# Weight tiles in pairs with seven block products instead of eight, and the mLSTM one head at a time, in a one-core decoder layer

## The chip, the core and the metric

The kernel runs on one core of a Trainium2 chip, as one program. The core has a matrix engine (PE in the rows; PEld is its loading of weights, which overlaps), a vector engine (DVE), a scalar engine (ACT), a general engine (POOL), and a queue engine (SP) that issues most transfers. SBUF is the working memory, PSUM holds matmul results in eight banks of 512 float32 columns by 128 partitions. The metric is the time of one execution in device microseconds; lower is better.

## The reference

One inference step of a hybrid decoder layer for 544 tokens: 512 of a new sequence and 32 new tokens of eight running sequences. In float32:

```
z = x @ w_in        # conv gates and input b, c, h; q, k, v, o; gates i, f; merge gates gc, gm
y_conv = (b * short_conv(c * h)) @ w_conv_out
h_m, C, n, m = mlstm_chunkwise(q, k, v, i, f, C0, n0, m0)     # 4 heads of 256, chunks of 128
y_m = (headnorm(h_m) * g * sigmoid(o)) @ w_m_out
x1 = layer_norm(alpha * x + (sigmoid(gc) * y_conv + sigmoid(gm) * y_m) @ w_o)
x2 = layer_norm(alpha * x1 + square(relu(x1 @ w_ff1)) @ w_ff2)
```

The width is 1024, the MLP 4096 wide. A chunk of the mLSTM takes the state matrix C (256x256) that the chunk before it left. The eight running sequences each have a C of every head that is read, used and written back, which is called the decode here.

## The kernel before, in words

All activations are held transposed: 128 features on the partitions, 8 such groups (`KT = 8`), 544 tokens along the free axis. The weights are cut into 160 tiles of 128 output features, each [128, 1024]: eight blocks of 128x128. Float32 accuracy comes from splitting every operand of the big products into a high and a low part: `wsplit_` (lines 136 to 142) loads a tile as `wr`, copies it on ACT into `wh` (L140) and subtracts on DVE into `wl` (L141). `mm` (L144 to L153) then runs, for each of the eight blocks, three products (high x high, high x low, low x high) on two halves of 272 tokens: 48 matmuls of 272 columns for a tile, all recorded at L151, into a two-bank PSUM tile `ps`.

The stages in program order are: gates and the first k tiles; q, o, v; the mLSTM of the prompt, by chunks, with the four heads inside a chunk; the decode, 32 slices `cr` of the state; the short convolution (24 tiles); its output product; the merge; the product with `w_o`; first norm; four rounds of MLP (eight tiles of the first matrix, eight of the second); second norm. A scheduler orders each engine's queue: it may interleave stages, so the mLSTM stands in the matrix engine's queue among the products of other tiles. Where a norm follows, the weights stay resident and the first half of the tokens goes through all eight tiles before the second half (`half`), so that the norm of one half has products beside it. Heads need DVE and ACT work in a chain: scores `S`, masked into `pm`, output `n` from `pm` and from the `state`, and the state's update `u`:

```
nc.vector.scalar_tensor_tensor(state[:, h, dt], state[:, h, dt],
                               dec[:, h, ch:ch + 1], pu[:, :257], op0=ALU.mult, op1=ALU.add)
```

In the decode each slice is loaded (`cr`), split (`ch` on ACT, `cl` on DVE, L492 and L493), used by matmuls `pq`, updated from matmuls `us` (L509 on DVE), and stored by a transfer that POOL issues. Six buffers of `cr` turn. POOL else does little: the mask `km`, a few products, and the low parts of eight tiles in the first round of the MLP (L141 and L611 with `eng` set to it).

Of the kernel before, what the change touches and what calls it, by code (L numbers as in the profile page):

```python
# [8 lines left out]
F32 = mybir.dt.float32  # L9
# [3 lines left out]
PSUM = bass.MemoryType.PSUM  # L13

P = 128
SEQ = 512
# [5 lines left out]
HW = 288               # tokens of the first part where the last norm follows  # L22
KT = 8
NH = 4
# [7 lines left out]
# columns of the packed small operands  # L32
# [10 lines left out]
# order of the weight tiles  # L43
W_K, W_Q, W_O, W_V, W_CONV, W_YC, W_GC, W_GM, W_OUT, W_FF = 0, 8, 16, 24, 32, 56, 64, 72, 88, 96


@with_exitstack
def tile_hybrid(ctx: ExitStack, tc: tile.TileContext, xT, wt, wg, pk, caug,
# [7 lines left out]
    wp = pool("wp", 3)  # L56
    slots = pool("slots")
    tmp = pool("tmp", 2)
    psa = pool("psa", 4, space=PSUM)
    pstate = {}  # L60

    def products_psum(n):
        """four banks for the products: two tiles of two, or four of one"""
        if pstate:
            pstate["stack"].close()
        pstate["stack"] = st = ExitStack()
        pstate["pool"] = pool(f"psm{len(pstate)}", n, stack=st, space=PSUM, reuse_waits="tile")

    ctx.callback(lambda: pstate["stack"].close())
    products_psum(2)  # L70
# [7 lines left out]
    def slot(i, pl=slots):  # L78
        return pl.tile([P, KT, NT], F32, name=f"slot{i}", tag=f"slot{i}")

    def r(ap):
        return ap.bitcast(F32R)

# [6 lines left out]
    ident = col("ident")  # L90

# [1 line left out]
    warm = cst.tile([P, P], F32, name="warm")  # L93
    nc.gpsimd.memset(warm, 0.0)
    pwm = aux("pwm")
    for j in range(9):
        nc.tensor.matmul(pwm[:, :P], warm, warm, start=True, stop=True)
    xh, xl = slot(0), slot(1)
    wgr = wp.tile([P, KT * P], F32, name="wgr", tag="wr")[:, :KT * 64]
    wgs = wp.tile([P, KT, P], F32R, name="wgs", tag="wh")  # L100
    early = {}

    def wload(i):
        raw = wp.tile([P, KT * P], F32, name=f"wr{i}", tag="wr")
        nc.sync.dma_start(raw, wt[i])
        return raw

    xr = slot(3)
    nc.sync.dma_start(wgr, wg)
    for kt in range(KT):  # L110
        nc.sync.dma_start(xr[:, kt], xT[:, kt])
        if kt == 1:
            early[0] = wload(0)
    early[1] = wload(1)
    for kt in range(KT):
        if kt == 0:
            w3 = wgr.rearrange("p (k m) -> p k m", k=KT)
            nc.scalar.copy(wgs[:, :, :64], w3)
            nc.vector.tensor_tensor(wgs[:, :, 64:], w3, wgs[:, :, :64].bitcast(F32),
                                    op=ALU.subtract)  # L120
        nc.scalar.copy(r(xh[:, kt]), xr[:, kt])
        nc.vector.tensor_tensor(r(xl[:, kt]), xr[:, kt], xh[:, kt], op=ALU.subtract)
    nc.sync.dma_start(pkt, pk)

    hv = (slice(0, HN), slice(HN, NT))

    ahead = {}

    def wsplit(i, eng=nc.vector):
        return ahead.pop(i) if i in ahead else wsplit_(i, eng)  # L130

    def split_ahead(*ii):
        for i in ii:
            ahead[i] = wsplit_(i)
# [9 lines left out]
    def mm(ps, wh, wl, ah, al, halves=hv, m=P, mid=None):  # L144
        for kt in range(KT):
            if kt == 5 and mid:
                mid()
            ws = slice(kt * m, (kt + 1) * m)
            for (w, a) in ((wh, ah), (wh, al), (wl, ah)):
                for hf, cs in enumerate(halves):  # L150
                    nc.tensor.matmul(ps[:m, hf, :cs.stop - cs.start], w[:, ws], r(a[:, kt, cs]),  # L151
                                     start=(kt == 0 and w is wh and a is ah),
                                     stop=(kt == KT - 1 and w is wl))  # L153

    def mtile(i, ah, al):
        wh, wl = wsplit(i)
        ps = pstate["pool"].tile([P, 2, 512], F32, name=f"ps{i}", tag="mm")
        mm(ps, wh, wl, ah, al)
        return ps

    def pv(ps):
        return ps[:, :, :HN]

    def hview(ap):
        return ap.rearrange("p (a n) -> p a n", a=2)

    mstk = ExitStack()          # what the mLSTM keeps to its end
# [5 lines left out]
    vk = mst.tile([P, NH, VW], F32, name="vk")  # L173
    nc.gpsimd.memset(G, 0.0)
    nc.gpsimd.memset(vk[:, :, 256:258], 0.0)
    nc.gpsimd.memset(vk[0:32, :, 256:257], 1.0)
    nc.gpsimd.memset(vk[64:96, :, 256:257], 1.0)

# [1 line left out]
    pstk = ExitStack()          # what only the prompt's mLSTM needs  # L180
    mg = pool("mg", stack=pstk)
    gstk = ExitStack()
    gr = pool("gr", stack=gstk)
    split_ahead(0, 1)
    gp = [aux(f"gp{hf}") for hf in range(2)]
    for kt in range(KT):
        for a in (xh, xl):
            for hf in range(2):
                nc.tensor.matmul(gp[hf][:, :HN], wgs[:, kt], r(a[:, kt, hv[hf]]),
                                 start=(kt == 0 and a is xh), stop=(kt == KT - 1 and a is xl))  # L190
# [4 lines left out]
    c = mg.tile([4, NT], F32, name="c")  # L195
# [5 lines left out]

    def sm(ap, n=DT):
        return ap.rearrange("p (b t) -> p b t", t=n)
# [8 lines left out]

    kT = slot(2)

    def ktile(ft):
        ps = mtile(W_K + ft, xh, xl)
        nc.scalar.activation(hview(kT[:, ft]), pv(ps), AF.Copy, scale=DH ** -0.5)

    for ft in range(3):
        ktile(ft)  # L220
# [29 lines left out]
    # rows that matmuls spread over the partitions, in exact halves: c, w_inter of the prompt  # L250
    R = mg.tile([P, SEQ], F32R, name="R")
    Rf = R.bitcast(F32)
    wrow = gr.tile([68, SEQ], F32, name="wrow")
    selr = mst.tile([P, 8], F32R, name="selr")
# [19 lines left out]
    gstk.close()  # L274
    mp = pool("mp", stack=pstk)
    E = mp.tile([P, NC, NH, P], F32, name="E")
    va = mp.tile([P, NC, NH, 257], F32, name="va")
    nc.gpsimd.memset(va[:, :, :, 256:257], 1.0)

    for ft in range(3, 6):  # L280
        ktile(ft)
# [34 lines left out]
    for ft in range(6, KT):  # L316
        ktile(ft)
# [159 lines left out]
    for t in qms:  # L477
        nc.gpsimd.memset(t, 0.0)
# [449 lines left out]
```

## Time and profile before

| | |
|---|---|
| time of three runs, us | 1104.53, 1100.12, 1102.09; median 1102.09 |
| the profiled execution, first to last instruction, us | 1099.7 |
| busy: PE, DVE, ACT, POOL, us | 1071.2, 535.5, 347.9, 143.0 |
| mean granted clock of the matrix engine, as a share of 2.4 GHz | 0.988 |
| moved by transfers | 110.37 MB, mean 100 GB/s |

The page shows no time of its own for the profiled execution beyond its span. An engine's busy time is the union of its instructions, so for the matrix engine, whose instructions overlap, the pace is read from counts over a stretch and not from the mean of one. In rows of windows an entry such as `100.00 (x800)` is the busy time of an engine and its instructions in that stretch; in rows of the timeline `x3` means three like instructions that follow each other, and the second number is the time from the first's start to the last's end.

### The profile page before, as it was taken

How to read it: one execution, taken by the hardware profiler on the slowest of the kernel's cores; microseconds unless marked ns; L12 is line 12 of the kernel's file. 1: busy time of each engine (PE TensorE's matmuls, PEld its weight loads, DVE VectorE, ACT ScalarE, POOL GpSimd, SP SyncE). 2: the span in 40 equal slices, each digit the busy share in tenths (PEclk: the TensorE clock that was granted, in tenths of full speed). 3: DMA queues.
4: the chain of work that ended last, by engine and by line, in shares of the span. 5: the costliest groups of instructions: out<-in, count | busy, mean ns of one | idle time of the engine just before them, and what ended most of it. 6: DMA issues, size and time to landing. Idle time of an engine off the chain costs nothing.

```text
span 1099.7 us, 19420 instructions
## 1 busy us (share of the span) xinstructions
PE 1071.2 (97%) x8351; PEld 1060.0 (96%) x8351; DVE 535.5 (49%) x882; ACT 347.9 (32%) x516; POOL 143.0 (13%) x161
## 2 busy tenths in 40 slices
PE   8999999999999989999999999899999999999994
PEld 8999999999999989999999999899999999999994
DVE  5533223365578778522143359742344234334576
ACT  6431222232234334213222225441233133123432
POOL 1000230000017563003200004200000000000033
PEclk9999999999999999999999999899999999999997
DMA  6222222211136775222222342112222222222201
GB/s 233 98 78 77 97 83 90 77 45 53 40 135 203 241 209 162 95 96 77 97 79 95 123 171 96 58 58 75 80 97 77 97 81 93 94 80 97 96 23 60
DMA packets 34349, 110.37 MB, mean 100 GB/s; under 512 B 3928, under 2 KB 6232, under 8 KB 34008
## 3 DMA queue, kind: packets, MB, share of 16 engines
q1 hardware_dynamic: 31704, 100.69, 28.2%
q0 software_dynamic: 2560, 8.46, 2.0%
q8 instruction: 65, 1.06, 0.4%
q14 instruction: 20, 0.16, 0.1%
HBM read 97.32 MB, written 11.81 MB: 99 GB/s over the span
## 4 chain that ended last, share of the span: by engine, by line
PE 90%; DVE 4%; DMA 3%; ACT 1%; issue 1%; POOL 0%; SPq 0%; DVEq 0%; POOLq 0%; ACTq 0%
PE ps L151 82%; DMA cr<-in_caug_dram 1%; DMA out_cs_dram<-cr 1%; PE u L419 1%; PE pq L496 1%; PE n L405 1%; DVE slot L733 1%; PE S L386 1%; PE n L402 1%; DMA wr<-in_wt_dram 1%; DVE bq L743 1%; DVE slot L671 0%; PE us L507 0%; PE ht L367 0%; PE kt L412 0%
## 5 line engine op out<-in xcount | busy, mean ns | idle before, releaser
L151 PE MATMUL ps<-slot,wh 128*128 128x272 f32 (+1 forms) x4640 | 801.2, 290 | 3.9 <-DVE slot L671 1.8
L151 PEld LDWEIGHTS ps<-slot,wh 128*128 128x128 f32 x4640 | 669.0, 189 | 7.0 <-DVE slot L671 2.5
L151 PE MATMUL ps<-slot,wl 128*128 128x272 f32 (+1 forms) x2320 | 498.2, 289 | 0.0
L151 PEld LDWEIGHTS ps<-slot,wl 128*128 128x128 f32 x2320 | 371.6, 189 | 0.7
L140 ACT CAST wh<-wr 128x1024 fp32r<-128x1024 f32 x145 | 152.1, 1050 | 501.1 <-PE ps L151 437.3
L141 DVE TENSOR_TENSOR wl<-wr,wh 128x1024 fp32r<-128x1024 f32 x142 | 174.1, 1226 | 205.8 <-ACT wh L140 201.7
L151 PE MATMUL ps<-slot,res 128*128 128x272 f32 (+2 forms) x720 | 92.8, 289 | 0.0
L151 PEld LDWEIGHTS ps<-slot,res 128*128 128x128 f32 x720 | 91.3, 188 | 0.3
L726 POOL TENSOR_TENSOR slot<-slot,bc 128x288 f32<-128x288 f32 (+1 forms) x6 | 5.8, 992 | 360.2 <-ACT bc L724 360.2
L810 DVE TENSOR_TENSOR slot<-ps,slot 128x544 f32<-128x544 f32 x16 | 11.6, 725 | 59.3 <-PE ps L151 59.3
L503 POOL TENSOR_SCALAR km<-kk,pkt 128x256 fp32r<-128x256 f32 x32 | 37.3, 1168 | 14.6 <-PE us L507 7.8
L492 ACT CAST ch<-cr 128x516 fp32r<-128x516 f32 x32 | 19.9, 623 | 49.6 <-DMA cr<-in_caug_dram 28.7
L785 ACT CAST slot<-rl 128x544 fp32r<-128x544 f32 (+1 forms) x40 | 22.2, 556 | 37.2 <-DVE rl L784 37.1
L786 DVE TENSOR_TENSOR slot<-rl,slot 128x544 fp32r<-128x544 f32 (+1 forms) x40 | 24.4, 611 | 19.6 <-ACT slot L785 19.4
L509 DVE SCALAR_TENSOR_TENSOR cr<-cr,dec,us 128x258 f32<-128x258 f32 x64 | 29.3, 475 | 3.3 <-PE us L507 3.1
L324 POOL TENSOR_SCALAR slot<-slot,pkt 128x544 f32<-128x544 f32 x8 | 16.8, 2096 | 107.9 <-ACT slot L323 107.9
L493 DVE TENSOR_TENSOR cl<-cr,ch 128x516 fp32r<-128x516 f32 x32 | 22.1, 697 | 17.6 <-ACT ch L492 17.5
L784 DVE TENSOR_TENSOR rl<-rl 128x544 f32<-128x544 f32 (+1 forms) x40 | 24.3, 607 | 11.8 <-ACT rl L783 11.8
L570 POOL TENSOR_TENSOR slot<-slot,sgc 128x544 f32<-128x544 f32 x8 | 14.5, 1809 | 88.1 <-ACT sgc L569 88.1
L783 ACT ACTIVATE rl<-ps 128x544 f32<-128x544 f32 (+1 forms) x40 | 21.2, 529 | 14.3 <-PE ps L151 14.3
L496 PE MATMUL pq<-ch,qm 128*64 128x258 f32 x64 | 18.3, 292 | 5.9 <-ACT wh L140 3.2
L141 POOL TENSOR_TENSOR wl<-wr,wh 128x1024 fp32r<-128x1024 f32 x3 | 7.3, 2423 | 124.9 <-PE am L645 121.2
(258 smaller groups left out, 715.2 us busy)
## 6 DMA issues: line engine op xcount, KB each, us to landing
wr<-in_wt_dram SPq DMA_DIRECT2D x160, 512.0 KB, 3.5
cr<-in_caug_dram SPq DMA_DIRECT2D x32, 258.0 KB, 3.9
out_cs_dram<-cr POOLq DMA_DIRECT2D x32, 258.0 KB, 3.9
slot<-in_xT_dram SPq DMA_DIRECT2D x8, 272.0 KB, 6.3
slot<-in_xT_dram SPq DMA_DIRECT2D x1, 2176.0 KB, 8.5
out_yT_dram<-slot SPq DMA_DIRECT2D x4, 288.0 KB, 2.4
out_cp_dram<-state SPq DMA_DIRECT2D x1, 1028.0 KB
out_yT_dram<-slot SPq DMA_DIRECT2D x4, 256.0 KB, 2.3
```

The source lines that it names most:

```text
L140: nc.scalar.copy(hi, raw)
L141: eng.tensor_tensor(lo, raw, hi.bitcast(F32), op=ALU.subtract)
L151: nc.tensor.matmul(ps[:m, hf, :cs.stop - cs.start], w[:, ws], r(a[:, kt, cs]), start=(kt == 0 and w is wh and a is ah), stop=(kt == KT - 1 ...
L492: nc.scalar.copy(r(chh), cr)
L493: nc.vector.tensor_tensor(r(cl), cr, chh, op=ALU.subtract)
L496: nc.tensor.matmul(pq[:2 * NS, :VW], r(qm[:, dt, bb * 2 * NS:(bb + 1) * 2 * NS]), r(part[:, dt]), start=(bb == 0 and dt == 0 and part is chh),
L503: nc.gpsimd.tensor_scalar(r(km), kk[:, 2 * h:2 * h + 2].rearrange("p a d -> p (a d)"), col("bsel")[:, bb:bb + 1], None, op0=ALU.mult)
L509: nc.vector.scalar_tensor_tensor(cr[:, dt], cr[:, dt], dec[:, h, 4 + bb:5 + bb], pu[:, :VW], op0=ALU.mult, op1=ALU.add)
L783: nc.scalar.activation(view(rl_), src, AF.Relu)
L784: nc.vector.tensor_tensor(rl_, rl_, rl_, op=ALU.mult)
L785: nc.scalar.copy(r(dh[:, ft, cs]), rl_)
L786: nc.vector.tensor_tensor(r(dl[:, ft, cs]), rl_, dh[:, ft, cs], op=ALU.subtract)
```

## The change

144 of the 160 tiles are processed in pairs. A pair is seen as a 2x2 block matrix (two output tiles by two halves of the input features), the activations as another (two halves of the features by two halves of the tokens), and the product is formed by a scheme that takes seven block products instead of eight: a block product is now 4 blocks x 3 high/low products = 12 matmuls of 272 columns, so a pair has 84 matmuls where two tiles had 96. The scheme needs sums of weight blocks (`wpair`: S1 to S4, on POOL), sums of activation blocks (`tsums`: T1 to T4, on POOL or DVE) and sums of results (`spair`, in PSUM and with ACT and DVE). Each operand is split into high and low parts after the sums. The 16 tiles of `w_o` and of the last round's second matrix stay as they were.

The activations now take 7 blocks for 4, so SBUF is laid out anew: the mLSTM runs head by head (projections of a head, `mlstm(h)`, `decode(h)`), with one buffer for most of its tiles, four for `cr`, and three PSUM banks for everything that is not a product (there were four); head outputs and gates go to DRAM and are loaded when they are merged. The low part `cl` moves from DVE to POOL, the mask `km` from POOL to ACT, the decode's stores from POOL's queue to SP's. Of the first norm only the first half has products beside it; the second half's norm is now run before the pairs of the MLP, which need all four token-by-feature blocks and their sums.

```diff
-    def wsplit_(i, eng=nc.vector):
-        raw = early.pop(i) if i in early else wload(i)
-        hi = wp.tile([P, KT * P], F32R, name=f"wh{i}", tag="wh")
-        lo = wp.tile([P, KT * P], F32R, name=f"wl{i}", tag="wl")
-        nc.scalar.copy(hi, raw)
-        eng.tensor_tensor(lo, raw, hi.bitcast(F32), op=ALU.subtract)
+    def wpair(i0, i1):
+        a, b = wload(i0), wload(i1)
+        H = KH * P
+        s = wp.tile([P, 3 * H], F32, name=f"ws{i0}", tag="ws", bufs=1)
+        s2, s1, s4 = (s[:, k * H:(k + 1) * H] for k in range(3))
+        a1, a2, b1, b2_ = a[:, :H], a[:, H:], b[:, :H], b[:, H:]
+        tt = nc.gpsimd.tensor_tensor
+        tt(s1, b1, b2_, op=ALU.add)
+        tt(s2, s1, a1, op=ALU.subtract)
+        tt(b1, a1, b1, op=ALU.subtract)
+        tt(s4, a2, s2, op=ALU.subtract)
+        g1 = halves(f"{i0}a", a)
+        g2 = halves(f"{i0}b", s[:, :2 * H])
+        g3 = halves(f"{i0}c", b)
+        g4 = halves(f"{i0}d", s4)
...
+    def tsums(nm, z, eng):
...
+        t = tmp["tt"].tile([P, 4, HN], F32, name=f"tt{nm}", tag="tt", bufs=1)
+        x1_ = z[:, 0].rearrange("p (a n) -> p a n", a=2)
+        x2_ = z[:, :, HN:]
+        eng.tensor_tensor(t[:, 0:2], x2_, x1_, op=ALU.subtract)
+        eng.tensor_tensor(t[:, 2], z[:, 1, HN:], t[:, 0], op=ALU.subtract)
+        eng.tensor_tensor(t[:, 3], z[:, 1, :HN], t[:, 2], op=ALU.subtract)
+        return t
...
+    def prod(ps, w, X, which, start):
+        set_, k = which
+        ah, al = X[set_ + "h"], X[set_ + "l"]
+        wh, wl = w
+        for kt in range(KH):
+            ws = slice(kt * P, (kt + 1) * P)
+            for n, (w_, a) in enumerate(((wh, ah), (wh, al), (wl, ah))):
+                nc.tensor.matmul(ps[:, :HN], w_[:, ws], r(a[:, kt, k]),
...
+        A = mmt(f"A{nm}")
+        prod(A, w["W11"], X, X11, True)
+        p1 = part("p1", A)
+        step()
+        F = mmt(f"F{nm}")
+        prod(F, w["W12"], X, X21, True)
+        ev.c11(F[:, :HN], p1)
+        step()
+        prod(A, w["S2"], X, T2, False)
+        q = part("q", A, 2)
+        D = mmt(f"D{nm}")
+        prod(D, w["S1"], X, T1, True)
+        prod(A, w["S3"], X, T3, False)
+        w_ = part("w", A)
+        ev.c22(D[:, :HN], w_)
+
+        def t0():
+            prod(A, w["W22"], X, T4, False)
+            ev.c21(A[:, :HN])
+
+        def t1():
+            prod(D, w["S4"], X, X22, False)
+            ev.c12(D[:, :HN], q)
+            ev.done()
...
+    for h in range(NH):
+        kT = kT0 if h == 0 else proj_k(h)
+        qT = qT0 if h == 0 else proj_q(h)
+        va, vk = proj_v(h)
+        flush()
+        mlstm(h, kT, qT, va)
+        decode(h, kT, qT, vk)
...
-        later[0], later[1] = first, second
...
+        if hf == 0:
+            later[1], later[2] = first, second
+        else:
+            Xa.update({k: o2.tile([P, KH, 4, HN], F32, name=f"a{k}", tag=k) for k in ("th", "tl")})
+            first()
+            second()
```

Here `halves` is the pair copy on ACT, subtract on DVE that `wsplit_` had, for 1024 columns (g1, g2, g3) or 512 (g4), recorded at L119 and L120 of the changed kernel; `step` runs the two last block products of the pair before. In the MLP a pair of the first matrix also squares its four results (three of them on DVE, L971) and ends with `tsplit`, the seven blocks of the next operand; a pair of the second matrix adds three partial results on POOL (L1000).

The matrix engine's queue in the mLSTM before: state updates `u` of head 0 to 3 in one chunk, with products of a weight tile (`ps`, L151) between them.

```order
L419 MATMUL u_1_1_2273<-va,kw_2249 128x257
L151 MATMUL ps_3529<-slot_87,wh_3525 128x272
L151 MATMUL ps_3529<-slot_86,wl_3526 128x272 x2
L151 MATMUL ps_3529<-slot_86,wh_3525 128x272 x2
L419 MATMUL u_2_0_2276<-va,kw_2249 128x257
L419 MATMUL u_2_1_2279<-va,kw_2249 128x257
L151 MATMUL ps_3529<-slot_87,wh_3525 128x272
L151 MATMUL ps_3529<-slot_86,wl_3526 128x272 x2
```

The same engine's queue after the change, in the mLSTM of the last head: it begins behind the last matmul of the decode of the head before (`hts`), and runs through the chunks.

```order
L629 MATMUL hts_2496<-pkt,nsbs_2478 128x32 x2
L335 MATMUL vp_0_2878<-pkt,vt_2723 128x128 x4
L507 MATMUL S_2898<-qT_2600,kT_2503 128x128 x8
L522 MATMUL n_0_2914<-va_2724,pm_2907 128x257
L539 MATMUL u_0_0_2925<-va_2724,kw_0_2917 128x257
L539 MATMUL u_0_1_2928<-va_2724,kw_0_2917 128x257
L522 MATMUL n_1_2931<-va_2724,pm_2907 128x257
L525 MATMUL n_1_2931<-state_2913,qT_2600 128x257
L539 MATMUL u_1_0_2936<-va_2724,kw_0_2917 128x257
L525 MATMUL n_1_2931<-state_2913,qT_2600 128x257
L539 MATMUL u_1_1_2939<-va_2724,kw_0_2917 128x257
```

(Rows between these that are transposes or the spread of a weight are left out.) Between the `vp` matmuls of the third head and the end of the fourth head's decode stand two products of weight tiles, and none behind those two; the queue goes on with the second pair of the convolution. By that place 1104 of the 6816 products have stood in the queue: 300 ahead of the first head's `vp`, 526 up to the second's, 276 up to the third's, and those two.

POOL's queue before, from the last product of the merge (`sgc`) to the second norm (`bc`): eight low parts of weight tiles in the first MLP round, and then nothing for the rest of the MLP.

```order
L570 TENSOR_TENSOR slot_4886<-slot_4886,sgc_5784 128x544
L141 TENSOR_TENSOR wl_7284<-wr_7281,wh_7283 128x1024
L141 TENSOR_TENSOR wl_7290<-wr_7287,wh_7289 128x1024
L611 TENSOR_TENSOR res_4_7299<-wr_7300,res_4_7299 128x1024
L611 TENSOR_TENSOR res_7_7317<-wr_7318,res_7_7317 128x1024
L726 TENSOR_TENSOR slot_6739<-slot_6739,bc_10721 128x288 x3
```

(Of the three rows of L141 two stand, of the five of L611 two.) POOL's queue after, for one pair of the first MLP matrix: the four weight sums (`ws`, and `wr` overwritten), then the sums of the hidden activations (`ttd` from `hid`).

```order
L130 TENSOR_TENSOR ws_8426<-wr_8424 128x512
L131 TENSOR_TENSOR ws_8426<-ws_8426,wr_8422 128x512
L132 TENSOR_TENSOR wr_8424<-wr_8422,wr_8424 128x512
L133 TENSOR_TENSOR ws_8426<-wr_8422,ws_8426 128x512
L152 TENSOR_TENSOR ttd_1_8372<-hid_1_8147 128x544
L153 TENSOR_TENSOR ttd_1_8372<-hid_1_8147,ttd_1_8372 128x272
L154 TENSOR_TENSOR ttd_1_8372<-hid_1_8147,ttd_1_8372 128x272
```

What moved: POOL has these seven for each such pair, where it had nothing for most of the MLP, and four for every other pair.

## Rows read from the trace of the kernel before

**Rows 1.** The page: busy time by engine, then the ending chain by engine.

```profile
PE 1071.2 (97%) x8351; PEld 1060.0 (96%) x8351; DVE 535.5 (49%) x882; ACT 347.9 (32%) x516; POOL 143.0 (13%) x161
...
PE 90%; DVE 4%; DMA 3%; ACT 1%; issue 1%; POOL 0%; SPq 0%; DVEq 0%; POOLq 0%; ACTq 0%
```

**Rows 2.** Windows: busy time (instructions) by engine, granted clock, DMA share, GB/s.

```profile
0.00:20.00 20.00, 17.15 (x100) 15.99 (x101) 9.71 (x17) 10.74 (x17) 2.94 (x22) 0.91 0.75 269
...
320.00:440.00 120.00, 114.14 (x901) 112.50 (x899) 93.92 (x201) 50.56 (x78) 65.18 (x82) 0.99 0.64 200
...
560.00:660.00 100.00, 100.00 (x800) 100.00 (x799) 41.94 (x54) 27.80 (x32) 0.00 (x0) 1.00 0.35 119
680.00:700.00 20.00, 15.72 (x93) 14.38 (x93) 19.45 (x28) 11.61 (x22) 7.74 (x4) 0.83 0.31 108
```

**Rows 3.** Groups by line and form: shapes, count, busy us, mean ns, idle before.

```profile
L141 DVE TENSOR_TENSOR wl<-wr,wh 128x1024 fp32r<-128x1024 f32 x142 | 174.1, 1226 | 205.8 <-ACT wh L140 201.7
L140 ACT CAST wh<-wr 128x1024 fp32r<-128x1024 f32 x145 | 152.1, 1050 | 501.1 <-PE ps L151 437.3 <-issue 61.5 <-DMA wr<-in_wt_dram 1.8
```

**Rows 4.** Timeline of DVE: instructions that follow each other without a wait.

```profile
551.00 1.22 DVE L141 TENSOR_TENSOR wl<-wr,wh 128x1024 fp32r<-128x1024 f32 x1
552.13 0.72 DVE L556 TENSOR_TENSOR slot<-sgm,slot 128x544 fp32r<-128x544 f32 x1
...
674.45 0.43 DVE L636 SCALAR_TENSOR_TENSOR ar0n<-av,ar0n 128x272 f32<-128x272 f32 x1
674.80 0.43 DVE L691 TENSOR_TENSOR as<-as,slot 128x272 f32<-128x272 f32 x1
```

**Rows 5.** Timeline of POOL: two instructions by themselves, two stretches beside DVE.

```profile
498.31 1.36 POOL L570 TENSOR_TENSOR slot<-slot,sgc 128x544 f32<-128x544 f32 x1 [60.10 <-ACT sgc L569]
...
665.46 2.40 POOL L141 TENSOR_TENSOR wl<-wr,wh 128x1024 fp32r<-128x1024 f32 x1 [1.07 <-ACT wh L140]
...
1074.53 2.75 POOL L726 TENSOR_TENSOR slot<-slot,bc 128x256 f32<-128x256 f32 x3 [6.52 <-ACT bc L724]
...
1087.82 2.49 POOL L759 TENSOR_TENSOR slot<-slot,bms 128x512 f32<-128x512 f32 x2 [7.08 <-ACT bms L756]
```

**Rows 6.** Timeline of DVE in the same stretches as the POOL rows.

```profile
665.65 2.50 DVE L691 TENSOR_TENSOR as<-slot 128x272 f32<-128x272 f32 x1
...
669.17 0.44 DVE L691 TENSOR_TENSOR as<-as,slot 128x272 f32<-128x272 f32 x1
...
1074.48 3.95 DVE L733 TENSOR_TENSOR slot<-slot,bc 128x256 f32<-128x256 f32 x5 [0.99 <-ACT bc L724]
...
1088.36 1.27 DVE L759 TENSOR_TENSOR slot<-slot,bm 128x512 f32<-128x512 f32 x2
```

**Rows 7.** Timeline of PE: six state-update matmul records in a row.

```profile
230.66 1.47 PE L419 MATMUL u<-va,kw 128*128 128x257 f32 x6
```

**Rows 8.** Groups by form in the mLSTM and the decode.

```profile
L493 DVE TENSOR_TENSOR cl<-cr,ch 128x516 fp32r<-128x516 f32 x32 | 22.1, 697 | 17.6 <-ACT ch L492 17.5
L492 ACT CAST ch<-cr 128x516 fp32r<-128x516 f32 x32 | 19.9, 623 | 49.6 <-DMA cr<-in_caug_dram 28.7 <-PE pq L496 8.1 <-PE ps L151 7.6
...
L424 DVE SCALAR_TENSOR_TENSOR state<-state,dec,u 128x257 f32<-128x257 f32 x24 | 10.8, 480 | 5.3 <-PE u L419 5.1
...
L389 DVE TENSOR_TENSOR pm<-S,E 128x512 f32<-128x512 f32 x4 | 2.8, 690 | 3.2 <-PE S L386 3.2
```

**Rows 9.** The page: transfers by group, KB each, median us to landing.

```profile
cr<-in_caug_dram SPq DMA_DIRECT2D x32, 258.0 KB, 3.9
out_cs_dram<-cr POOLq DMA_DIRECT2D x32, 258.0 KB, 3.9
```

**Rows 10.** Timeline of PE: matmuls behind a gap in the decode.

```profile
404.98 0.31 PE L496 MATMUL pq<-ch,qm 128*64 128x258 f32 x1 [3.16 <-ACT wh L140]
...
405.87 0.63 PE L507 MATMUL us<-vk,km 128*128 128x258 f32 x2
...
407.84 1.04 PE L151 MATMUL ps<-slot,wh 128*128 128x272 f32 x4
```

More of the change, by code (lines that the diff above doesn't have):

```diff
@@ L13 @@
 PSUM = bass.MemoryType.PSUM
+DRAM = bass.MemoryType.DRAM
 P = 128
@@ L55, in tile_hybrid @@
     cst = pool("cst")
[L56 to L70, printed above, removed]
+    wp = pool("wp")
+    stg = pool("stg")
+    o1 = pool("o1")
+    dr = pool("dr", space=DRAM)
+    psa = pool("psa", 3, space=PSUM)
+    psm = pool("psm", 5, space=PSUM)
     def tables(name):
@@ L90, in tile_hybrid @@
     ident = col("ident")
[L93 to L101, printed above, removed]
+    hD = dr.tile([P, KT, NT], F32, name="hD")
+    yD = dr.tile([P, KT, NT], F32, name="yD")
+    gD = dr.tile([P, KT, NT], F32, name="gD")
@@ L144, in mm @@
[L144 to L153, printed above, removed]
@@ new lines, in tile_hybrid, with __init__, part, add @@
+    class Evac:
+        def __init__(self, z, scale=None, done=None):
+            self.z, self.scale, self.then = z, scale, done
+        def part(self, t, ps):
+            if self.scale is None:
+                nc.scalar.copy(t, ps)
+            else:
+                nc.scalar.activation(t, ps, AF.Copy, scale=self.scale)
+        def add(self, out, ps, t):
+            if self.scale is None:
+                nc.vector.tensor_tensor(out, ps, t, op=ALU.add)
+            else:
+                nc.vector.scalar_tensor_tensor(out, ps, self.scale, t, op0=ALU.mult, op1=ALU.add)
+        def c11(self, ps, t):
+            self.add(self.z[:, 0, :HN], ps, t)
+        def c22(self, ps, t):
+            self.add(self.z[:, 1, HN:], ps, t)
+        def c12(self, ps, t):
+            self.add(self.z[:, 0, HN:], ps, t)
+        def c21(self, ps):
+            self.part(self.z[:, 1, :HN], ps)
+        def done(self):
+            if self.then:
+                self.then()
@@ L172, in tile_hybrid @@
     Es = mst.tile([NS, NH, NS], F32, name="Es")
-    vk = mst.tile([P, NH, VW], F32, name="vk")
-    nc.gpsimd.memset(G, 0.0)
[L175 to L184, printed above, removed]
-    gp = [aux(f"gp{hf}") for hf in range(2)]
[L186 to L190, printed above, removed]
+    R = mst.tile([P, SEQ], F32R, name="R")
@@ new lines, in tile_hybrid @@
+    E = mst.tile([P, NC, NH, P], F32, name="E")
+    wb = mst.tile([P, 2, NH, NS], F32, name="wb")
+    selr = mst.tile([P, 8], F32R, name="selr")
+    epst = cst.tile([P, 1], F32, name="epst")
+    hp = pool("hp", 2, stack=mstk)
+    gstk = ExitStack()
+    tmp["tt"] = gr = pool("gr", stack=gstk)
+    warm = gr.tile([P, P], F32, name="warm")
+    nc.gpsimd.memset(warm, 0.0)
+    nc.gpsimd.memset(G, 0.0)
+    nc.gpsimd.memset(epst, EPS)
+    pwm = aux("pwm")
+    for j in range(9):
+        nc.tensor.matmul(pwm[:, :P], warm, warm, start=True, stop=True)
@@ new lines, in tile_hybrid @@
+    kT0 = proj_k(0)
+    w3 = wgr.rearrange("p (k m) -> p k m", k=KT)
+    nc.scalar.copy(wgs[:, :, :64], w3)
+    nc.vector.tensor_tensor(wgs[:, :, 64:], w3, wgs[:, :, :64].bitcast(F32), op=ALU.subtract)
+    gp = [aux(f"gp{hf}") for hf in range(2)]
+    for hf, terms in enumerate((((0, X11), (KH, X21)), ((0, X11), (KH, X22), (0, T1)))):
+        seq = [(o + kt, X[s_ + hl][:, kt, k]) for o, (s_, k) in terms for kt in range(KH)
+               for hl in "hl"]
+        for n, (kt, a) in enumerate(seq):
+            nc.tensor.matmul(gp[hf][:, :HN], wgs[:, kt], r(a), start=(n == 0),
+                             stop=(n == len(seq) - 1))
@@ L272, in tile_hybrid @@
     nc.sync.dma_start(m_o, mo)
[L274 to L281, printed above, removed]
+    qT0 = proj_q(0)
     for ch in range(NC + 1):
@@ L573, in tile_hybrid @@
[L573 to L585 removed]
+    n = NU - 2
```

781 lines of the change are left out of this document (437 added, 344 removed).

## The prediction

> **What bounds the kernel now.** I read the page first: the matrix engine is busy for 1071.2 us of a span of 1099.7, and 90% of the ending chain is its own [rows 1]. DVE is at half of the span and POOL at an eighth. Then the windows [rows 2]: from 560 to 660 us 800 products start in 100 us, 125 ns each, without a gap, while POOL does nothing. So a tile's 48 products cost 6.0 us and two tiles 12.0, and what else a tile needs (a copy of 1.05 us, a subtract of 1.23 [rows 3]) is hidden. Two stretches differ. In the decode (320 to 440) the matrix engine is busy for 114 of 120 us; behind the first norm (680 to 700) it runs 93 products where 160 fit, with a granted clock of 0.83. A change that shortens products is therefore worth their count, until another engine needs longer for a pair than the products do; that is what I looked for next.
>
> The sum is made against the profiled execution's 1099.7 us. The median of the runs, 1102.1, is 2.4 more, which is added at the end.
>
> **Products.** 72 pairs have 84 products for 96: 72 x 12 x 0.125 = 108 us less. A pair's products now take 10.5 us. This is the only saving.
>
> **What DVE and POOL need for a pair.** The scheme adds POOL work, and the trace shows that POOL and DVE are not independent. By themselves, POOL took 1.36 us for 544 columns and 2.40 for 1024, and 1.245 for 512 [rows 5]: 2.4 ns a column, so 0.66 for 272. On DVE, 1024 columns with two SBUF operands take 1.13 from start to start and 272 take 0.35 [rows 4]; by the line through these, 512 take 0.60, 544 take 0.63 and 1088 take 1.20. But a DVE instruction of 272 columns that began beside a POOL product took 2.50 us: it started 0.19 after POOL's and ended 0.29 after it, where a like one took 0.44 [rows 5, 6]. And where three POOL and five DVE instructions of 256 columns ran together, POOL's took 0.92 each and DVE's 0.79 [rows 5, 6]. By the lines POOL's would be 0.61 and DVE's 0.33. A pair of them then has 0.95 us of work, and takes 0.92 at POOL's pace. So they hardly overlap. Where DVE's other operand was in PSUM it kept its pace beside POOL: two of 512 columns in 1.27 [rows 5, 6]. I therefore add the prices of POOL's instructions and of DVE's with two SBUF operands, multiply by 0.95, and compare with 10.5.
>
> The Trainium skill ("SBUF — State Buffer", section "Who interferes with whom") calls the port pair that DVE and GpSimd share an exclusive lock; the rows agree but for 0.92 against 0.95. By the lock in full, without the factor 0.95, the sum would be 30 us higher; that is rival three.
>
> A pair without other work: DVE's subtracts are three of 1024 and one of 512, 3.99 us; POOL's four sums of 512 are 4.98. Together 8.97, by the factor 8.5: hidden under 10.5.
>
> A pair of the first MLP matrix has in addition three squares of 272 (1.05), the low parts of 544, 272 and 1088 (2.18), and POOL's activation sums of 544, 272, 272 (2.68): 14.88, by the factor 14.1. Twelve such pairs (three rounds of four) are 3.6 over 10.5: **43 us**. A pair of the second matrix adds three POOL sums of 272 to the plain pair, 10.95 or 10.4: nothing over. The last round's four have no activation sums and fewer parts, about 10.6: nothing.
>
> Three convolution pairs have 26.9 for weights and 11.1 for POOL's product of 1024, four taps, the gate, low parts and sums: 38.0, by the factor 36.0, over 31.5. About three and a half of the four such groups stand behind the mLSTM, where nothing else fills the time: **15 us**. The four pairs of `o` have a product of 1088, low parts and sums: 15.0, by the factor 14.2, 15 us over; the four plain pairs of `gm` behind them give back up to 2 us each: **7 us**. The merge's four have three of 1088: 12.6, by the factor 11.9: **6 us**.
>
> This term is 71 us. Below, it is 0 if weights split ahead and the two engines' gaps absorb it; above, 101 without the factor, and 130 as an outer bound if the instructions also wait for one another in their chains.
>
> **The mLSTM head by head.** Before, the state updates of several heads stood in the matrix engine's queue among products [the first order rows]. Now 1102 of the products stand ahead of the third head's `vp`, and two behind it until the fourth head's decode ends; the next pairs need space that the mLSTM frees. So the third and fourth heads run with almost no cover. One head: the prompt's four chunks need about 21 us, some 6 to the first state (scores, mask 0.69, transposes), three further chunks of 3.2 (ten float32 matmul records of about 0.22, as six take 1.47 less the last one's tail [rows 7], and two state updates of 0.48 [rows 8]), and about 5 for head norm and transposes, six to ten steps of 0.48 to 0.69 [rows 8]. The decode has eight slices through four buffers instead of 32 through six: load 3.9 [rows 9], `ch` 0.62 [rows 8], `cl` 1.27 on POOL by its pace, matmuls and updates about 1, store 3.9 [rows 9] make a turn of 10.6 for four slices, about 20 for eight. Together 42, of which the matrix engine works about 18.5 (36 records of 0.22, some 90 smaller at 0.11 to 0.125). It idles 23.5 per head, 47 for two. The second head has 276 products (34 us) in its 42, so about 9 more. Before, the decode idled 6 [rows 2], which go. **+50 us**. Below 20, if a head's decode overlaps the next head's prompt; above 90, if the chains' steps also wait for DVE's and POOL's weight work.
>
> What the change moves without a wait of its own: the mask from POOL to ACT, the decode's stores from POOL's queue to SP's. On SP a store stands ahead of later loads of `cr` and of weights; that is within the decode's turn above. Head outputs and gates through DRAM add a few MB where the transfers move 119 GB/s in a product stretch and 269 at the start [rows 2]: nothing.
>
> **The other places.** The second half's norm now stands before the first pair of the MLP with nothing beside it. Before, 680 to 700 lost 67 of 160 products, 8.4 us [rows 2]; after, the chain of sums, root, scale, sums of blocks and split I take as 20 us: **+12**, between 5 and 25. At the start a pair needs all of `x` and two tiles, 3.3 MB at 269 GB/s [rows 2], 12 us, then four sums through one buffer: **+7**, between 2 and 15. At the four seams between the MLP's matrices the last hidden tile's squares, sums and split (about 6 us) have 58 products (7 us) beside them, which the pair's last two block products only partly are: 2 each, **+8**, between 0 and 16.
>
> Sum: -108 + 71 + 50 + 12 + 7 + 8 = +40. 1099.7 + 40 is 1139.7; with 2.4, **1142 us**, 3.6% slower.
>
> **The rivals.**
> One, faster: DVE and POOL have slack that I do not count, since weights can be split ahead during light pairs and their instructions interleave better than in the rows. For it: DVE is at 49% now and POOL at 13% [rows 1]. Against it: the 2.50 us of [rows 6]. The first term goes from 71 to 0: 1071. The kernel is faster when this term is below 31 with the others as they stand. Chance 0.2.
> Two, no change: both large terms come out at a little over half (71 to 41, 50 to 37, the start and seams hidden): about 1098 to 1103. Chance 0.08.
> Three, much slower: the clock falls in the uncovered heads, or the two engines exclude each other entirely. For the clock: behind a gap of 3.16 us two like matmuls take 0.63 and four products 1.04 to the end of the last [rows 10], so about 0.2 us from one to the next instead of 0.125, and 680 to 700 has 0.83 [rows 2], a mixture of 2.4 and 1.2 GHz. The work of the two uncovered heads, 37 us, would take twice as long: +35, so 1177. The exclusion without the factor gives +30, 1172. Chance 0.22.
> The Trainium skill ("TensorE: Matmul & The Clock Gate", section "Why this matters for your kernels") says that idle gaps between bursts of matmuls put the clock back to its lower level; rows 10 agree, and by this rule alone rival three would be the likelier.
>
> **How the numbers follow.** My forecast, 1142 with a range of its own from 1110 to 1165, has 0.5. What a measurement of this kernel can tell from no change is about 0.5%, 5.5 us. Faster by more than that is rival one, 0.2; within it is rival two, 0.08; slower is the forecast and rival three, 0.72. The range that leaves out no more than 2 in 10 reaches from 1075, near rival one, to 1200, above rival three with both of its causes in part.
>
> **What the profile after would show.** If the exclusion is right: the sums at L130 to L133 at 1.2 us or longer and DVE's subtracts at L120 well above 1.13 in their mean, both engines together near full in the MLP rounds, and a window of 100 us in them with about 620 to 700 products instead of 800. If rival one holds, the windows have 800, and POOL and DVE overlap. If the head term is right, the matrix engine idles for about 45 us between the third head's first product and the second convolution pair, waiting for DVE and for `cr`; the granted clock there decides rival three. The windows behind the first norm and at the start show the smaller terms. I would be wrong on the sign if DVE and POOL had no such stretch, and wrong on the size most likely in the heads, where no row shows a head alone.

## The result, and the profile after

The changed kernel takes **1264.3 us** (median of four runs, 1260.4 to 1266.9), the kernel before 1102.6: a ratio of **1.1475**, interval 1.1442 to 1.1508. It is nearly 15% slower. I had forecast slower by 3.6%, 1142 us, with a range up to 1200; the direction was right, the size was not, and the time lies 64 us above the range.

The page of the changed kernel: busy time by engine, then the ending chain by engine (against [rows 1]).

```profile
PE 1063.9 (84%) x7487; PEld 1009.3 (80%) x7487; DVE 917.8 (73%) x1263; ACT 566.9 (45%) x946; POOL 701.6 (56%) x488
...
DVE 11%; PE 10%; POOL 6%; issue 5%; DMA 2%; ACT 2%; DVEq 0%; POOLq 0%; ACTq 0%
```

The shares of the second line are of the whole span, and they add up to 36%: the chain's first piece begins at 813.3 us, and ahead of it nothing was followed. So its 10% is not to be set against the 90% of before; in the part that was followed, the MLP, DVE and POOL have 17% together and the matrix engine 10%. Over the whole execution DVE or POOL is busy for 1098 of 1261.5 us. The matrix engine's own busy time hardly fell (1071 to 1064) though 864 products are gone. The windows of the changed kernel (columns as in [rows 2]) show where the time goes:

```profile
0.00:40.00 40.00, 26.01 (x113) 22.68 (x114) 24.81 (x30) 16.82 (x25) 20.70 (x37) 0.68 0.38 135
250.00:338.00 88.00, 59.06 (x279) 44.59 (x278) 45.39 (x141) 30.47 (x64) 23.13 (x19) 0.77 0.37 119
366.00:476.00 110.00, 92.94 (x670) 90.42 (x669) 94.23 (x107) 48.78 (x79) 76.74 (x46) 0.94 0.23 76
576.00:597.00 21.00, 21.00 (x169) 21.00 (x168) 13.82 (x16) 11.82 (x18) 13.70 (x9) 1.00 0.39 130
786.00:845.00 59.00, 36.76 (x229) 33.74 (x228) 42.08 (x72) 29.71 (x58) 15.88 (x14) 0.80 0.10 36
915.00:1023.00 108.00, 93.04 (x671) 89.29 (x671) 79.52 (x85) 48.17 (x76) 83.47 (x56) 0.94 0.24 77
```

From 576 to 597 two pairs run their 168 products in 21 us, 125 ns each: here the scheme gives its whole 1.5 us a pair. Elsewhere it does not. Eight convolution pairs take 110 us for 84 (366 to 476). One MLP round, eight pairs, takes 108 (915 to 1023). At the start, in the third and fourth heads (250 to 338, 88 us for two) and behind the norm (786 to 845) the matrix engine is idle for 33 to 38% of the time, and its granted clock is 0.68 to 0.80.

What the weight sums cost is seen in the groups by form of the changed kernel: POOL's four sums, and one DVE line of the hidden tiles and one of the resident weights (which have no POOL sums beside them).

```profile
L133 POOL TENSOR_TENSOR ws<-wr,ws 128x512 f32<-128x512 f32 x72 | 138.4, 1922 | 0.0
L131 POOL TENSOR_TENSOR ws<-ws,wr 128x512 f32<-128x512 f32 x72 | 124.5, 1729 | 4.7
L132 POOL TENSOR_TENSOR wr<-wr,wr 128x512 f32<-128x512 f32 x72 | 116.4, 1617 | 0.0
L130 POOL TENSOR_TENSOR ws<-wr 128x512 f32<-128x512 f32 x72 | 106.4, 1478 | 295.5 <-DMA wr<-in_wt_dram 96.4
...
L971 DVE SCALAR_TENSOR_TENSOR hid<-hid 128x272 f32<-128x272 f32 x48 | 39.1, 819 | 0.8
...
L120 DVE TENSOR_TENSOR resl<-wr,resh 128x1024 fp32r<-128x1024 f32 x8 | 9.8, 1223 | 2.3 <-ACT resh L119 2.1
```

512 columns on POOL, 1.245 us unhindered [rows 5], take 1.48 to 1.92 in the mean; DVE's 272 columns, 0.44 [rows 6], take 0.82. Two stretches of the timeline of the changed kernel, DVE first, then POOL, show why:

```profile
1058.95 2.31 DVE L120 TENSOR_TENSOR wl131a<-wr,wh131a 128x1024 fp32r<-128x1024 f32 x1
1061.18 1.52 DVE L971 SCALAR_TENSOR_TENSOR hid<-hid 128x272 f32<-128x272 f32 x1
1062.63 2.39 DVE L159 TENSOR_TENSOR d2tl<-ttd,d2th 128x1088 fp32r<-128x1088 f32 x1
1064.94 2.31 DVE L120 TENSOR_TENSOR wl131b<-ws,wh131b 128x1024 fp32r<-128x1024 f32 x1
1067.17 0.43 DVE L247 TENSOR_TENSOR hid<-D,w 128x272 f32<-128x272 f32 x1
```

```profile
1058.63 1.54 POOL L130 TENSOR_TENSOR ws<-wr 128x512 f32<-128x512 f32 x1 [1.84 <-DMA wr<-in_wt_dram]
1060.25 2.15 POOL L131 TENSOR_TENSOR ws<-ws,wr 128x512 f32<-128x512 f32 x1
1062.37 1.50 POOL L132 TENSOR_TENSOR wr<-wr,wr 128x512 f32<-128x512 f32 x1
1063.83 2.33 POOL L133 TENSOR_TENSOR ws<-wr,ws 128x512 f32<-128x512 f32 x1
```

They take turns. DVE's subtract waits from 1058.95 for POOL's sum to end at 1060.17 and then runs 1.1; POOL's next sum starts at 1060.25, waits for DVE until about 1061.2 and ends at 1062.40; and so on. Only L247, whose first operand `D` is in PSUM, keeps its 0.43. Both engines are drawn as busy, and at any time one of them works.

### The profile page after: what moved, and what is told of

It is laid out like the page before. It is cut to its first block, busy times and chain, and to the rows that moved or that the text cites. A ratio compares the mean times of both kernels' runs of the same rounds, so it can differ in the third digit from the quotient of the medians.

```text
span 1261.5 us, 19444 instructions
## 1 busy us (share of the span) xinstructions
PE 1063.9 (84%) x7487; PEld 1009.3 (80%) x7487; DVE 917.8 (73%) x1263; ACT 566.9 (45%) x946; POOL 701.6 (56%) x488
## 5 line engine op out<-in xcount | busy, mean ns | idle before, releaser
L130 POOL TENSOR_TENSOR ws<-wr 128x512 f32<-128x512 f32 x72 | 106.4, 1478 | 295.5 <-DMA wr<-in_wt_dram 96.4
L133 POOL TENSOR_TENSOR ws<-wr,ws 128x512 f32<-128x512 f32 x72 | 138.4, 1922 | 0.0
L131 POOL TENSOR_TENSOR ws<-ws,wr 128x512 f32<-128x512 f32 x72 | 124.5, 1729 | 4.7
L132 POOL TENSOR_TENSOR wr<-wr,wr 128x512 f32<-128x512 f32 x72 | 116.4, 1617 | 0.0
L605 POOL TENSOR_TENSOR cl<-cr,ch 128x516 fp32r<-128x516 f32 x32 | 44.7, 1401 | 87.4 <-ACT ch L604 76.4
L241 ACT COPY p<-A 128x272 f32<-128x272 f32 x68 | 26.1, 384 | 48.5 <-PE A L183 37.4
L241 ACT COPY w<-A 128x272 f32<-128x272 f32 x68 | 25.9, 381 | 31.5 <-PE A L183 29.8
L971 DVE SCALAR_TENSOR_TENSOR hid<-hid 128x272 f32<-128x272 f32 x48 | 39.1, 819 | 0.8
L241 ACT COPY q<-A 128x272 f32<-128x272 f32 x68 | 25.9, 380 | 28.9 <-PE A L183 28.8
L152 POOL TENSOR_TENSOR ttd<-hid 128x544 f32<-128x544 f32 x12 | 25.3, 2110 | 21.8 <-DVE hid L971 19.4
L1000 POOL TENSOR_TENSOR x<-x,w 128x272 f32<-128x272 f32 x12 | 15.5, 1288 | 8.9 <-ACT w L241 8.9
```

The source lines that it names most:

```text
L130: tt(s1, b1, b2_, op=ALU.add)
L131: tt(s2, s1, a1, op=ALU.subtract)
L132: tt(b1, a1, b1, op=ALU.subtract)
L133: tt(s4, a2, s2, op=ALU.subtract)
L241: nc.scalar.copy(t, ps)
L605: nc.gpsimd.tensor_tensor(r(cl), cr, chh, op=ALU.subtract)
```

## The experiments

Each kernel is the changed one with the edit shown (in part, `...` for what is left out), unless it says otherwise. e1 to e6 and e12 ran once each. e1 to e4 are set against one run of the kernel before on the same chip, 1100.9 us, and against the changed kernel's 1264.3. The four runs of the changed kernel span 6.5 us, and the kernel before had 1099.7 to 1103.2 from chip to chip, so a difference of a few us between two single runs says nothing.

**e1: no sums of weight blocks.**

```diff
...
-        tt(s1, b1, b2_, op=ALU.add)
-        tt(s2, s1, a1, op=ALU.subtract)
-        tt(b1, a1, b1, op=ALU.subtract)
-        tt(s4, a2, s2, op=ALU.subtract)
         g1 = halves(f"{i0}a", a)
-        g2 = halves(f"{i0}b", s[:, :2 * H])
+        g2 = halves(f"{i0}b", a)
         g3 = halves(f"{i0}c", b)
-        g4 = halves(f"{i0}d", s4)
+        g4 = halves(f"{i0}d", b1)
```

> The four weight-block sums on POOL are left out (the seven block products run on plain blocks, so the outputs are not the reference's); everything else is as in the changed kernel. Theory A (POOL and DVE exclude each other, and the sum of their prices for a pair decides the pace): 72 x 4.98 = 359 us of excluded time goes, pairs of the first MLP matrix need 9.9 and convolution groups 23 us, under their products, so the waits between the heads and the first norm and in the MLP rounds go, and with them half of the slow-clock time: 1110 to 1150 us. Theory B (the waits stand at serial places, the seams between matrices, heads and norm, whatever POOL does): 1210 us or more.

Measured 1135.0: theory A. The four POOL sums of a pair cost 129 us, and A's 359 us of POOL time were two thirds hidden. One MLP round falls from 108 to 92.5 us; a window of e1 over it, to set against 915 to 1023 above:

```profile
831.00:924.00 93.00, 88.86 (x678) 86.59 (x677) 62.72 (x86) 48.77 (x77) 28.38 (x24) 0.98 0.29 93
```

From the first product of one stage to that of the next, the 129 us lie so: 21 up to the second convolution group, 25 in the convolution behind it, 7 in the yc and gc pairs, 17 in o and gm, 3 in the merge and the product with `w_o`, 46 in the first three MLP rounds and 9 from there to the end.

**e2: all sums on DVE.** `tt`, `tsums`, the added partial results (L1000) and the convolution's product (L668) get `nc.vector` for `nc.gpsimd`.

> All weight-block sums, activation sums, added partial results and the convolution's product move from POOL to DVE; nothing is left out. Theory A: DVE does them at 1.04 ns a column instead of POOL's 2.4 and nothing excludes it any more; a pair of the first MLP matrix then has 12.0 us on DVE alone (3.99 + 2.4 + 1.05 + 2.18 + 1.33 + 1.05) instead of 14.9 of both and 1.05 of PSUM adds, a plain pair 7.4: 1150 to 1190 us. Rival (DVE is simply the fuller engine, and POOL's work beside it is a help): DVE gets some 200 us more, and the time rises above 1264.

Measured 1163.2: theory A, 101 us faster with the same arithmetic. It is not POOL's slowness by itself that cost them: by my prices POOL alone needs 4.98 + 2.68 us for a pair of the first MLP matrix, 7.7, under the products' 10.5. In the groups of e2 DVE makes a sum in 0.68 to 0.71 us, and its 272 columns are back at 0.43:

```profile
L131 DVE TENSOR_TENSOR ws<-ws,wr 128x512 f32<-128x512 f32 x72 | 51.3, 712 | 0.4
...
L971 DVE SCALAR_TENSOR_TENSOR hid<-hid 128x272 f32<-128x272 f32 x48 | 20.3, 433 | 0.1
```

**e3: the layout with eight products.** Everything but the scheme: each pair multiplies its two plain tiles, and `t` holds the split of the fourth activation block instead of four sums.

```diff
+        def out(tag, k, c):
+            ps = mmt(f"{tag}{nm}")
+            prod(ps, w[f"W{k}1"], X, X11 if c == 1 else X12, True)
+            prod(ps, w[f"W{k}2"], X, X21 if c == 1 else X22, False)
+            return ps[:, :HN]
```

> The new layout and order alone: head by head, gates and head outputs through DRAM, second half of the first norm in front of the MLP, but each pair with its eight block products (96 matmuls) and no sums; nothing is left out of the result. Theory A: the layout alone loses in heads, norm, start and their slow clock some 75 to 100 us against the kernel before, 1175 to 1205 us, so that seven products save 108 and cost some 170 to 195 in DVE and POOL work and what follows from it. Rival (the layout is free, the scheme costs everything): within 15 us of 1102.

Measured 1163.7, 62.7 above the kernel before; 11 below A's window, far from the rival. A window of e3 over an MLP round:

```profile
851.00:947.00 96.00, 96.00 (x766) 96.00 (x765) 37.72 (x56) 29.88 (x48) 0.00 (x0) 1.00 0.27 89
```

Eight pairs of 96 products in 96.6 us, with no wait at the seam between the matrices. Counted as time beyond 125 ns a product, e3 loses 157 us up to its fifth convolution pair (at 343 us), behind all its heads, and the kernel before 105 up to the end of its decode (at 440): 52 more, the start included. Behind that e3 loses 10 more, 8 of them around the first norm. So the layout's 62.7 lie mostly in the heads and the norm, and the scheme, which takes 864 products (108 us) away, made the kernel 100.6 us slower on top of it.

**e4: the gate pairs in the fourth head.** The eight pairs of `gc` and `gm` are written in `decode`'s place of the fourth head, results through DRAM.

```diff
         mlstm(h, kT, qT, va)
+        for j in more[2 * h]:
+            gate_pair(j)
+        flush()
         decode(h, kT, qT, vk)
+        for j in more[2 * h + 1]:
+            gate_pair(j)
```

> The eight pairs of the two merge gates stand in the fourth head, two sets of four, both results through DRAM, so that products stand among the third and fourth heads' matmuls; arithmetic as in the changed kernel. Theory A: the heads' waits (9.8 + 12 + 9.1 us in 240 to 360) and the slow clock of their own matmuls (some 28 us over before) mostly go: 1205 to 1225 us. Rival (in the heads DVE is the bound, and products there only move the wait): 1245 us or more.

Measured 1238.5, 26 us less, between the two theories. The matrix engine is better filled from 240 to 390, but the seams ahead of the yc pairs and of the merge, where the same pairs had stood, got longer (from the first product of the last o pair to that of the second merge pair 36.9 us, where the products of two pairs need 21).

**e5: e2 and e4 together.**

> The second and fourth experiment together: all sums on DVE, and the eight gate pairs in the fourth head. Theory A (two separate losses): the 25 us of the gate pairs come off the 1163 of the DVE sums, 1130 to 1145 us. Rival (DVE is the bound in the heads as soon as it makes the sums): 1155 us or more.

Measured 1153.8: only 9 under e2, just below the rival's window. The gains do not add; with DVE's sums the gate pairs bring a third of what they brought.

**e6: a pair of the next round in each seam.** On e5.

```diff
+        if ck < 3:
+            z0 = ztile(f"hid{ck + 1}_0")
+            spair(i0 + 16, i0 + 16 + KH, Xa, Hidden(z0))
```

> As e5, and the first pair of the next MLP round stands ahead of each second matrix of the rounds one to three, so that 84 products that need nothing of the last hidden tile lie in the seam. Theory A (a round's loss of 10 us over its eight pairs' 84 is the wait for the last hidden tile's split and sums): rounds of 85 to 88 us instead of 94, 15 to 25 us under e5. Rival (DVE's work for a round sets its length): the wait moves elsewhere, within 8 us of e5.

Measured 1141.5, 12.3 under e5: more than the rival's 8, less than A's 15. A round falls from 94 to 90 us.

**e7: the first half of the tokens first.** On e6: three pairs run eight products; for both output tiles those on the first half of the tokens come first, and the sums T1 and the block X22 are needed only behind them. These pairs need no weight sums.

```diff
+        for ps, g, out in zip(pss, (g1, g2), (ev.e11, ev.c21)):
+            prod(ps, at(g, 1), X, X21, False)
+            out(ps[:, :HN])
...
+        def late(n, g, out, then=None):
+            ps = mmt(f"D{n}{nm}")
+            prod(ps, at(g, 1), X, X22, True)
+            prod(ps, at(g, 0), X, T1, False)
```

> As e6, and three pairs (the first k pair, the first two of the MLP) run eight block products in an order in which the first 48 need only the first half of the tokens and no sums; 36 products more. Theory A: they cover half of the wait behind the second half's norm and of the start, 15 to 30 us under e6, which would be 1075 to 1110 us, near or under the kernel before. Rival (DVE, which splits weights and norms the second half, is the bound there): within 8 us of e6.

Measured 1120.3, ratio 1.0161 (1.0125 to 1.0197): 21 under e6 as A has it, though it has 36 products more; above the time that A gave for the sum. How much of the 21 is the order, and how much the weight sums that three pairs no longer wait for, was not separated.

**e8: dummy products in the waits.** On the changed kernel.

```diff
+            for i in range(n):
+                tc.keep_in_program_order(nc.tensor.matmul(
+                    dm[:, :HN], w[:, :P], r(X["ph"][:, i % 3, 0]), start=(i == 0),
+                    stop=(i == n - 1)))
```

> The changed kernel with 228 products more, whose results nobody reads: 48 and 72 in the waits of the first norm's second half, 36 in the first wait of each second MLP matrix in the rounds one to three. Theory A (the slow clock behind a wait is paid on top of the wait): the granted clock behind these waits stays at its upper level, some 15 us of slow products there go, and the time is 5 to 20 us lower although work was added. Rival (the clock costs nothing there, since DVE decides the pace): the same time or up to 15 us more.

Measured 1261.7, ratio 1.1445 (1.1402 to 1.1487), against 1.1475: no difference. Two windows behind the norm: of the changed kernel from the first pair's first product on, of e8 from just ahead of the first dummy product (the first pair's own begin at 801.6):

```profile
786.00:838.00 52.00, 29.76 (x173) 26.74 (x172) 35.08 (x64) 25.61 (x50) 11.31 (x10) 0.77 0.06 21
```

```profile
793.00:845.00 52.00, 44.48 (x289) 41.79 (x290) 33.40 (x60) 22.66 (x44) 12.16 (x10) 0.87 0.07 21
```

The clock rises from 0.77 to 0.87, the matrix engine works 15 us more (the 120 dummies), and the stage is no shorter: from the last product of `w_o` to the first of the third pair it takes 51.3 us in the changed kernel and 53.7 in e8. So the rival's time came. Here a higher clock gave nothing back; that DVE sets the pace there fits, but is not shown by this run. The clock was raised in a part of the stage only: from 828 to 838 most of e8's products still follow each other at 0.23 us, as they do from 827 to 830 in the changed kernel.

**e9 to e11: how far it can be mended.** e9 and e10 are e7 with one gate pair left in each of the two seams and two pairs in each MLP seam; e9 pins the next head's pairs behind a head's scores, e10 does not; e11 is e10 with two gate pairs pinned in the fourth head.

```diff
+        with tc.issue_after(scores[h - 1]) if h else ExitStack():
             kT = kT0 if h == 0 else proj_k(h)
```

> As e7, with three moves of products and none of arithmetic: the matrix engine may take the three pairs of the next head only behind the scores of this one, and the gate pairs only behind the scores of the fourth, so that each head has 250 products or more beside it; one gate pair stays at each of the two seams ahead of the yc pairs and of the merge; two pairs of the next MLP round stand in a seam instead of one. Theory A (what is left over the products is waits at serial places, 92 us in e7, not the amount of DVE work): the heads' and seams' waits halve, 1075 to 1100 us, at or under the kernel before. Rival (DVE, at 83% of the span in e7, is the bound): 1110 us or more.

> As e9 without the pins in the heads, so that the fourth head runs without products again: e9's gain from the seams alone. Theory A: 10 to 20 us under e7's 1120 from the seams, given back in part by six instead of eight gate pairs in the heads (up to 20 us): 1110 to 1125 us. Rival as for e9: 1120 us or more.

> As e10, with two of the six gate pairs allowed only behind the scores of the fourth head, so that its 45 us have 264 products beside them; no pins elsewhere, since e9's pins on the pairs of the next head made each head longer. Theory A (e10 still lost some 25 us in the uncovered fourth head): 1088 to 1100 us, under the kernel before. Rival (what DVE needs for a head and for the pairs beside it adds up, so that covering a head only makes it longer): within 5 us of e10's 1109.

Measured 1131.7 (1.0274, interval 1.0229 to 1.0319), **1109.4** (1.0074, 1.0049 to 1.0099) and 1118.2 (1.0171, 1.0146 to 1.0196). e10 came just under A's window and is the best version, 0.7% behind the kernel before. e9 lies in the rival's window. e11 lies in neither: covering the head made the kernel 9 us longer, where the rival had no change within 5. Windows of the fourth head, from the last matmul of the third's decode to that of its own, of e10 and of e11:

```profile
321.00:366.00 45.00, 31.55 (x136) 24.21 (x136) 22.62 (x68) 14.65 (x31) 7.87 (x7) 0.73 0.31 100
```

```profile
305.00:377.00 72.00, 60.25 (x403) 55.88 (x403) 43.07 (x96) 36.17 (x60) 8.67 (x7) 0.86 0.37 119
```

With 264 products (33 us) beside it, the head takes 26 us longer, 71 for 45. These products had stood in the third head of e10, which becomes only 17 us shorter without them (504 products in 90 us, 240 in 73). The move loses 9, which is the whole difference between e10 and e11: what products cost beside a head depends on which head and where in its chain. That DVE's work for the pairs and the order within the matrix engine's queue both lengthen the head's chain is likely, but which has what share was not tried.

**e12: e6's and e7's moves with the sums left on POOL.**

> The changed kernel, sums on POOL as they were, with the two moves of e6 and e7 alone: the first pair of the next MLP round in each seam, and three pairs in the order that begins with the first half of the tokens. Theory A (serial places and exclusion are separate losses that add): the 12 and 21 us that the moves gave with DVE's sums come off 1264 as well, 1225 to 1238 us. Rival (with the sums on POOL the work of the two engines sets the length of the MLP rounds, so that covered seams only move the wait): the start's and the norm's part alone, 1240 to 1255 us.

Measured 1223.9, 40 under the changed kernel: theory A, and slightly more. As in e7, three pairs are also spared their weight sums, on POOL here. A window of e12 over the eight pairs of one round:

```profile
908.00:1011.00 103.00, 91.29 (x676) 88.79 (x675) 83.88 (x85) 48.14 (x76) 86.66 (x57) 0.95 0.25 82
```

That is nearly the exclusion by itself. With the seam covered the round takes 102.8 us, from 907.9 to 1010.7, and laying the two engines' instructions over each other, neither is busy for only 2.4, so one of the two works for 100.4. My prices give four pairs of 14.88 and four of 10.95, 103.3. In the changed kernel the same count for the round of 108.35 leaves 6.8 in which neither works. Some five of them lie in the seam and just behind it (975 to 1000). Rows of the timeline of the changed kernel there, in the next round; the matrix engine first, then DVE, then POOL:

```profile
1073.81 0.39 PE L183 MATMUL A<-d2ph,wh136a 128*128 128x272 f32 x1 [2.21 <-ACT wh136a L119]
1081.43 0.59 PE L183 MATMUL A<-d2ph,wl136a 128*128 128x272 f32 x1 [4.96 <-DVE wl136a L120]
```

```profile
1088.19 1.23 DVE L120 TENSOR_TENSOR wl136c<-wr,wh136c 128x1024 fp32r<-128x1024 f32 x1 [3.25 <-ACT wh136c L119]
```

```profile
1091.46 1.65 POOL L152 TENSOR_TENSOR ttd<-hid 128x544 f32<-128x544 f32 x1 [7.74 <-DVE hid L971]
```

The second matrix's first pair waits 5 us for a weight tile that the engines, behind with the hidden tiles, had not split ahead; then they wait in turn, POOL 7.7 us for the last hidden block, which the matrix engine could not finish sooner.

## Why the prediction was wrong, by its own steps

The runs give an account against 1100.9 us of the kernel before: the layout 62.7 (e3), products -108, weight sums on POOL 129.3 (changed kernel less e1), and 79.4 for the rest of the scheme, which is what remains of 163.4. Each term is known to a few us, and it holds in this order of taking things away; e4 and e5 show that not all gains add. Two steps failed by their size: the term for DVE and POOL, 58 us short, and the serial places (start, norm, seams), about as much.

- **Products, -108.** As forecast: light pairs take 10.5 us, those of e3 12.07.
- **The mLSTM, +50, and the second half's norm, +12.** Together 62, and e3 measures 62.7; in parts 52 with the start, and 8 at the norm. A head that I had put at 42 us takes 44: the window from 250 to 338 holds two. What the matrix engine does in it I had wrong: it is busy for 59 of the 88 us, where I had 37, its clock being low, and idle for 29, where I had 47. That the head's length came out right all the same suggests that its chain, and not that work, sets it.
- **DVE and POOL, +71: the first step that failed, by its size.** The weight sums alone cost 129, which is the outer bound that I had named, 130, and not the forecast. The mechanism was right, and rival one, that it would be absorbed, is refuted by e1 and e2. Where I had worked out a surplus I was near in the MLP (43 for the first matrix's pairs; e1 gives back 46) and in the merge (6 against 3), and low in the convolution (15 against 25) and in o and gm (7 against 17). And I had priced at nothing every place where a pair's sum stayed under 10.5: the pairs up to the second convolution group (21), yc and gc (7) and what follows the third MLP round (9). A likely reason is that a sum under 10.5 is hidden only if it can be done ahead, and the four split buffers hold one pair. Whether these 37 us are exclusion, or a pair's split waiting for four sums in a row through the one buffer `ws`, was not tried.
- **The factor 0.95** did not follow from its rows: 0.92 us for 0.95 us of work is 0.97. It is a small error. In the covered round of e12 one of the two engines works for 100.4 us against 103.3 by the full prices, again 0.97; with 0.95 it would be 98. At the full prices the term would have been 101, still short of 129. The Trainium skill ("SBUF — State Buffer", section "Who interferes with whom") has one engine hold the shared ports for a whole instruction while the other waits; the trace agrees to within 3%.
- **The start, +7, and the seams, +8: the second step that failed, far too small.** With the 108 us of products set aside, e1, where the weight sums have gone, takes 79 us more than e3, and I had 15. Counted as time beyond 125 ns a product, stage by stage, they lie so: some 24 from the start to the fifth convolution pair, of which 11 ahead of the second pair; 8 in yc and gc; 23 in `w_o` and behind the first norm, where the layout's 8 come on top, 31 for my 12; 23 in the MLP rounds, for my 8. A round of e1 takes 92.5 for 84, 8.5 more where I had 2: I had set 6 us of work on the last tile against 58 products and not asked whether the next matrix's weights would be ready. The moves of e6 and e7, which put other products into such places, gave 12 and 21 us, and 40 with the sums on POOL (e12).
- **The clock (rival three, +35).** It fell where I said, to 0.77 in the heads and 0.80 behind the norm. Behind the norm e8 raised it, in part of the stage, without a gain. In the heads it was not tried; two of them take 88 us, for 84 that I had without it and 119 with it. What of the 1064 us of the busy matrix engine is products drawn out by the clock, and would vanish without shortening anything, the rows don't say.

So the kernel is slower by mechanisms that I had named, at about twice their price. DVE and POOL, not the matrix engine, set the pace of the changed kernel's MLP rounds and convolution (neither works for 6.8 of 108 and 4.4 of 110 us), and even with every sum on DVE, the seams filled and three pairs reordered, the seven products only reach the eight of the kernel before (e10, 0.7% slower).

## What to carry to other kernels

A scheme that saves matmuls pays with sums and splits of operands. Add up, for each stage, what DVE and POOL need for them as if they were one engine wherever both read two operands from SBUF, at full price, and put the work on the faster one. Then look at each place where the next product needs the last one's result, and ask what has been prepared ahead and what else stands in the queue there; a stage whose average fits still loses at its seam. To learn which part of a large change costs what, run the layout without the new arithmetic and the arithmetic without its preparation: two runs gave most of this account.

## What the runs showed of the hardware that I had not expected

DVE and POOL hold each other up in both directions: POOL's 512 columns went from 1.245 us to as much as 1.92 in the mean, DVE's 272 from 0.43 to 0.82, while an instruction with an operand in PSUM kept its 0.43. The mean clock of one stage could be raised from 0.77 to 0.87 with dummy products, and the kernel did not become faster. And products put beside a dependent chain were not free: 33 us of them made the fourth head 26 us longer, and the third 17.
